# A one-core decoder trunk: squares in x's room, early evictions, finer strand steps, and strand work queued behind the FFN's operations

## The chip, the core and the metric

The kernel runs on one core of one Trainium2 chip. TensorE (PE) multiplies; VectorE (DVE), ScalarE (ACT) and GpSimd (POOL) do the elementwise work; SyncE (SP) and ScalarE issue the DMAs. Each engine runs its own instructions in order and waits on semaphores for the others. The metric is the device time of one execution in microseconds, median of several runs; less is better.

## The reference, cut to what matters

One layer of a hybrid decoder over 2,048 prompt positions and 8 samples, width 1,024, all in float32:

```
h = RMSNorm(x);  z = h @ W_in                 # W_in: 1024 x 2432
A = chunked gMLP(z_u, z_v)     B = S5 state space(z_b)
C = short gated convolution    D = RWKV-7 time mixing (4 heads of 64)
x = x + concat(A, B, C, D) @ W_out
gate, up = split(RMSNorm(x) @ W_gu);  x = x + (silu(gate) * up) @ W_down   # d_ff 2816
y = RMSNorm(x)                                # and the states as outputs
```

## The kernel before

**Pieces.** The positions are cut into four pieces `q` of 512 columns; the samples ride with one of them as 8 further columns. Activations lie transposed, features on partitions. A float32 product is made of three passes: operands are split in a rounded part (`hi`) and a bfloat16 rest (`lo`), and `mmg` (L272) emits hi*hi (L281), then lo*hi and hi*lo (L286). `weights` (L224) loads half a weight tile into a `raw` buffer (three of them), rounds it on ACT (L240), and either makes its rest on DVE (L244, the first time, and stores it) or loads the rest stored before (L242).

**Stages.** For piece 0, `norm0` loads x, scales it into `h` and starts the sum of squares; `m.columns()` (`zrw`) makes the seven z tiles of RWKV, the first four of which wait in PSUM (`mm`, four buffers) for the norm's factor `rs0`, which `zload` multiplies in (L790). `zrest` makes the other ten. Then for q = 1, 2, 3 `norm1(q)` (L403) and `park(h, q, n1)` (L749) compute all z tiles of that piece and store them to HBM (`zdr`), so that later `zload` only loads them. `norm1` loads each x tile into a buffer of the pool `gz` (tag "t", six buffers, shared with z tiles, with the park's `zp` and with the FFN's ft, gp and gr), writes `h` into ring side 1 (`put_gain`, L380), and squares x into a tile of tag "raw" (L415), the weights' own three buffers; `squares` (L302) adds four of these on POOL (L313) and the last three on DVE (L317, L319). `Rms`/`rms` (L327) then make 1/rms: matmuls with ones (L338), a square root on ACT, a reciprocal on DVE, a Newton step (L290) on POOL or DVE, and matmuls that broadcast it (L354).

**Main stream.** For each piece: `outphase` (W_out), `norm2`, `ffn`, and for the first three `final`. In `ffn`, `up(f)` is two weight tiles of matmuls (gate, up), `gated` (L1436) takes them through DVE gp, ACT tanh, POOL gr, DVE ft twice, ACT ah and DVE al (L1445 to L1451), and `down` adds products into x on DVE (L1464).

**Strands.** Work that is not a large matmul is written as generators. `tick` (L127) counts PE work (1 for a matmul of 512 columns); each `Strand` sleeps for as many ticks as it yields and then emits its next step in the middle of the main stream's matmuls. PE's order is this emission order, by hand. The order on DVE, ACT, POOL and the DMA queues is made by a list scheduler: in its own model of time it takes the ready instruction with the highest priority (main stream 8000, RWKV strand `RP` 4000, others `MP` 3500; among equals the earlier emitted). While the FFN of piece q runs, the strands of piece q+1 run: `Mix.rwkv` (two halves of `rw_a` to `rw_d`, with a triangular inverse of 30 dependent steps on POOL, L1256 to L1261) and `Mix.others` (`zrest`, gMLP, S5), which starts in the FFN at `i == 3`. In `zrest` for a parked piece everything up to the first `yield 0` is one step: 15 or 16 loads from `zdr` and their elementwise work. For piece 0, `s5_setup` (L506) makes tables with long chains on POOL (its powers in L651 to L677 use the same scratch `inv_` as the inverse), and eight rounds of PE transposes (L711) that need POOL copies (L699).

## Time and profile before

| | |
|---|---|
| three runs, median | 2643.06 us (2640.42 to 2652.55) |
| the profiled execution | 2647.65 us, its span 2645.9 us |
| TensorE clock granted over it | 0.955 of full |
| busy in the span | PE 92%, DVE 53%, ACT 40%, POOL 30% |

The span is the time between the first and the last instruction of the profile; the execution's own time is 1.75 us longer. PE is busy nearly always, so that what can be saved is its idle time and the stretches in which its clock was granted at half. Stages by the trace: piece 0's columns and the rest of its z tiles to 145 us, the three parks to about 640 us, then four rounds of `outphase` and FFN; strands run beside the first three, to about 2185 us.

### The profile page before, as it was taken

The page shows a single profiled execution, that of the slowest core. Times are in us where ns is not written, and L with a number is a line of the kernel's source. Part 1 is how long each engine was busy: PE and PEld are TensorE (multiplying, and loading weights), DVE is VectorE, ACT ScalarE, POOL GpSimd, SP SyncE. Part 2 cuts the span into 40 slices and gives each one's busy share as a digit, 9 for nine tenths or more (in the row PEclk, how much of TensorE's full clock was granted, in tenths as well). Part 3 has the DMA queues.
Part 4 walks back from the last instruction along what each step waited for, and adds up shares of the span by engine and source line. Part 5 has one row for each costly group of instructions (what it writes and reads, how often), then busy time and mean ns, then how long its engine had stood idle before and what let it go on. Part 6 is the DMA issues. An engine that isn't in the chain of part 4 may idle for free.

```text
span 2645.9 us, 39723 instructions
## 1 busy us (share of the span) xinstructions
PE 2422.5 (92%) x13857; PEld 1622.9 (61%) x14020; DVE 1414.7 (53%) x2790; ACT 1045.6 (40%) x2118; POOL 792.0 (30%) x1267
## 2 busy tenths in 40 slices
PE   7949979799979999999899999997999999999997
PEld 3638846555545556545466565554665558888886
DVE  6943233333788776656755554557555543333334
ACT  4542243433453333345533333544343435322223
POOL 6085116201263262032621711426235113100001
PEclk8978989899989999999999999998999999999999
DMA  5334546555444444464434544634444346444443
GB/s 170 112 115 145 174 133 192 162 155 181 120 126 126 134 138 129 131 185 141 147 120 125 156 128 138 214 110 146 128 135 145 109 141 203 130 134 134 137 138 99
DMA packets 285320, 375.86 MB, mean 142 GB/s; under 512 B 50968, under 2 KB 160576, under 8 KB 285120
## 3 DMA queue, kind: packets, MB, share of 16 engines
q1 hardware_dynamic: 239568, 323.19, 40.4%
q10 hardware_dynamic: 45552, 50.14, 5.4%
q8 instruction: 110, 1.80, 0.3%
q14 instruction: 90, 0.74, 0.1%
HBM read 318.89 MB, written 54.31 MB: 141 GB/s over the span
## 4 chain that ended last, share of the span: by engine, by line
PE 68%; POOL 10%; DVE 10%; issue 4%; DMA 4%; ACT 3%; ACTq 0%; SPq 0%; POOLq 0%; DVEq 0%
PE m L286 38%; PE m L281 21%; POOL BD L1261 3%; POOL inv L1259 3%; DMA z<-zdr 1%; PE x L1229 1%; DVE wl L244 1%; PE x L1305 1%; PE x L1296 1%; PE x L1285 1%; POOL rs L313 1%; POOL s5Q L520 1%; ACT wh L240 1%; DVE U L834 1%; PE ms L717 1%
## 5 line engine op out<-in xcount | busy, mean ns | idle before, releaser
L286 PE MATMUL m<-rl,wh 128*128 128x512 bf16 (+1 forms) x2758 | 847.4, 340 | 13.0 <-DVE rl L384 3.5
L286 PE MATMUL m<-rh,wl 128*128 128x512 bf16 (+1 forms) x2641 | 826.6, 347 | 0.1
L240 ACT CAST wh<-raw 128x512 fp32r<-128x512 f32 x744 | 451.7, 618 | 945.1 <-PE m L286 585.1
L281 PE MATMUL m<-rh,wh 128*128 128x512 f32 (+1 forms) x2760 | 652.5, 377 | 78.7 <-ACT wh L240 63.3
L286 PEld LDWEIGHTS <-wl 128*128 128x128 bf16 x3640 | 353.0, 100 | 350.9 <-issue 106.2
L281 PEld LDWEIGHTS m<-rh,wh 128*128 128x128 f32 x2760 | 455.2, 194 | 177.8 <-ACT wh L240 65.1
L286 PEld LDWEIGHTS <-wh 128*128 128x128 bf16 x3640 | 359.1, 99 | 237.1 <-issue 17.2
L1447 POOL TENSOR_TENSOR gr<-gp,rs 128x512 f32<-128x512 f32 (+1 forms) x110 | 124.9, 1144 | 749.3 <-DVE gp L1445 680.3
L1464 DVE TENSOR_TENSOR xm<-m,xm 128x512 f32<-128x512 f32 (+1 forms) x440 | 246.9, 581 | 128.4 <-PE m L286 119.0
L281 PE MATMUL m<-ah,wh 128*128 128x512 f32 (+1 forms) x880 | 250.8, 401 | 56.7 <-DVE gp L1445 16.0
L286 PE MATMUL m<-al,wh 128*128 128x512 bf16 (+1 forms) x880 | 275.9, 344 | 3.8 <-issue 1.3
L286 PE MATMUL m<-ah,wl 128*128 128x512 bf16 (+1 forms) x838 | 267.5, 351 | 0.7 <-DMA wl<-lod 0.7
L281 PEld LDWEIGHTS m<-ah,wh 128*128 128x128 f32 x880 | 149.2, 193 | 108.0 <-DVE xm L1464 19.1
L1259 POOL TENSOR_TENSOR inv<-BD 32x30 f32<-32x30 f32 (+14 forms) x240 | 132.3, 551 | 197.0 <-DMA BD<-dl 178.8
L244 DVE TENSOR_TENSOR wl<-raw,wh 128x512 bf16<-128x512 f32 x186 | 139.3, 757 | 59.9 <-ACT wh L240 56.4
L1445 DVE TENSOR_TENSOR gp<-m,rs 128x512 f32<-128x512 f32 (+1 forms) x110 | 62.1, 582 | 175.9 <-PE m L286 148.6
L1261 POOL TENSOR_TENSOR BD<-BD,inv 32x30 f32<-32x30 f32 (+14 forms) x240 | 148.4, 618 | 18.2
L1284 POOL TENSOR_SCALAR stl<-st,g 128x64 f32<-128x64 f32 x128 | 68.5, 549 | 276.6 <-DVE st L1299 256.3
L1448 DVE SCALAR_TENSOR_TENSOR ft<-ft,gr 128x512 f32<-128x512 f32 (+1 forms) x110 | 78.7, 730 | 83.6 <-POOL gr L1447 70.6
L1449 DVE SCALAR_TENSOR_TENSOR ft<-ft,m 128x512 f32<-128x512 f32 (+1 forms) x110 | 62.0, 580 | 99.8 <-PE m L286 98.8
L1451 DVE TENSOR_TENSOR al<-ft,ah 128x512 bf16<-128x512 f32 (+1 forms) x88 | 63.2, 718 | 35.9 <-ACT ah L1450 35.3
L757 DVE TENSOR_TENSOR zp<-m,rs 128x260 f32<-128x260 f32 (+1 forms) x68 | 35.8, 554 | 85.3 <-PE m L286 72.7
(378 smaller groups left out, 2677.3 us busy)
## 6 DMA issues: line engine op xcount, KB each, us to landing
raw<-in_wgu SPq DMA_DIRECT2D x352, 256.0 KB, 2.9
wl<-lod SPq DMA_DIRECT2D x558, 128.0 KB, 2.2
raw<-in_wd SPq DMA_DIRECT2D x176, 256.0 KB, 2.9
raw<-in_wz SPq DMA_DIRECT2D x136, 256.0 KB, 2.9
lod<-wl ACTq DMA_DIRECT2D x186, 128.0 KB, 3.2
raw<-in_wo SPq DMA_DIRECT2D x64, 256.0 KB, 3.3
zdr<-zp ACTq DMA_DIRECT2D x40, 256.0 KB, 2.9
z<-zdr SPq DMA_DIRECT2D x40, 256.0 KB, 3.7
```

The costliest lines, as they stand in the source:

```text
L240: S.copy(hi, raw)
L244: V.tensor_tensor(lo, raw, hi.bitcast(F32), op=ALU.subtract)
L281: T.matmul(p_[:, :n], lhsT=wh, rhs=xh[:, c0 : c0 + n], start=i == 0, stop=False)
L286: T.matmul(p_[:, :n], lhsT=a, rhs=b[:, c0 : c0 + n], start=False, stop=e and i == ends[id(ps)])
L1259: G.tensor_tensor(tv, xtv[:, 0:s, s : s + 1].to_broadcast([32, s, r]), xtv[:, s : s + 1, s + 1 :].to_broadcast([32, s, r]), op=ALU.mult)
L1261: G.tensor_tensor(xtv[:, 0:s, s + 1 :], xtv[:, 0:s, s + 1 :], tv, op=ALU.add)
L1284: G.tensor_scalar(stl[:, j], old[:, j], pvw[:, 8 * j + c, 32:33], None, op0=ALU.mult)
L1445: V.tensor_tensor(gp[:, c], pss[0][b][:, :n], rs[:, c], op=ALU.mult)
L1447: G.tensor_tensor(gr[:, c], gp[:, c], rs[:, c], op=ALU.mult)
L1448: V.scalar_tensor_tensor(tv, tv, 1.0, gr[:, c], op0=ALU.add, op1=ALU.mult)
L1451: V.tensor_tensor(al[:, :w], t[:, :w], ah[:, :w].bitcast(F32), op=ALU.subtract)
L1464: V.tensor_tensor(xm[m][:, c0 : c0 + n], p_[:, :n], xm[m][:, c0 : c0 + n], op=ALU.add)
```

## The change

- `Strand.step`: the step's instructions on ACT and DVE are queued behind the main stream's last FFN operation already emitted on that engine (`anchors`): ah on ACT; al, or the last addition of `down`, on DVE. `issue_after` orders the queue of one engine and adds no semaphore.
- `squares` in `norm1` writes the square over x itself, so that "raw" holds weights only; for q = 1 x lies in the two large tiles `big0`, `big1` (which `norm0` used before, and `rw_b` uses after), and `norm1(1)` is emitted right after piece 0's columns instead of after `zrest`.
- The Newton steps of the first norm and of `norm1` go from POOL to DVE.
- In `zrw` for piece 0, the first two z tiles are copied by ACT from PSUM to SBUF before the norm is done, and scaled in place later.
- Steps: `zrest` of a parked piece yields 12 ticks at up to 15 more places; `s5_setup` 28 for 20; `norm2`'s strand waits 48 for 30, `final`'s 100 for 40; `nx.start(36)` for `nx.start(10)`.

```diff
--- before.py
+++ after.py
@@ -93,6 +93,7 @@
     offs = [0]
     strands = []
     now = [0.0]
+    anchors = {}
 
     class hp:
 
@@ -116,7 +117,11 @@
             strands.append(self)
 
         def step(self):
-            with hp(self.prio):
+
+            with ExitStack() as es:
+                es.enter_context(hp(self.prio))
+                for a in anchors.values():
+                    es.enter_context(tc.issue_after(a.ins))
                 d = next(self.gen, None)
             if d is None:
                 self.over = True
@@ -307,8 +312,9 @@
             if k == 0:
                 act(acc[:, :w], xk(k), AF.Square)
                 continue
+            x = xk(k)
             sq = new()
-            act(sq[:, :w], xk(k), AF.Square)
+            act(sq[:, :w], x, AF.Square)
             if not fast or k < 5:
                 G.tensor_tensor(acc[:, :w], acc[:, :w], sq[:, :w], op=ALU.add)
             elif late is None:
@@ -405,23 +411,25 @@
         w = zwidth(q)
         h = ring_tile(1)
 
+        xs = []
+
+        big = [rw.tile([P, 4 * TW], F32, tag=f"big{i}", name=nm("x1")) for i in range(2)] if q == 1 else []
+
         def xk(k):
-            t = zt_("x")
+            t = big[k // 4][:, TW * (k % 4) : TW * (k % 4) + TW] if big else zt_("x")
             nc.sync.dma_start(t[:, :w], I["xq"][q, :, k, :w])
             put_gain(h, k, w, t[:, :w], "n1")
+            xs.append(t)
             return t[:, :w]
 
-        def sq():
-            return wpool.tile([P, TW], F32, tag="raw", bufs=3, name=nm("sq"))
-
-        return h, Rms(squares(xk, w, sq, True), w, prio=MP, wait=64, gap=48)
+        return h, Rms(squares(xk, w, lambda: xs[-1], True), w, V, prio=MP, wait=64, gap=48)
 
     early = [weights([("wz", 0)], (60000, 49999))[0]]
     with hp(20000):
         h, acc0 = norm0()
 
-    first = Rms(acc0, TP, wait=60, prio=18000)
-    rs0 = acc0
+    first = Rms(acc0, TP, V, wait=60, prio=18000)
+    rs0 = acc0[:, :TP]
 
 
     glu = cload("glu", [P, 2, 256])
@@ -703,7 +711,7 @@
                         else:
                             act(cv[ps_, ri, g], bc[ps_, 3, pr], AF.Copy, scale=-1.0)
                             act(fv[ps_, ri, :, g], Ft[ps_, 1, pr], AF.Copy, scale=-1.0)
-                yield 40 if pr == 0 else 20
+                yield 40 if pr == 0 else 28
                 yield from ms_free()
                 pe = mst()
                 pm = pe[:, 256:384]
@@ -782,19 +790,29 @@
     ahead0 = []
 
     def zload(h, m, q, off=0):
-        t = zt_()
         if q in parked:
+            t = zt_()
             nc.sync.dma_start(t[:, off : off + zwidth(q)], zdr[q - 1, m, :, : zwidth(q)])
             return t
-        for p_, (c0, n) in zip(ahead0.pop(0) if ahead0 else ztile(h, m, q), zblocks(q)):
-            V.tensor_tensor(t[:, off + c0 : off + c0 + n], p_[:, :n], rs0[:, c0 : c0 + n], op=ALU.mult)
+        p_ = ahead0.pop(0) if ahead0 else ztile(h, m, q)[0]
+        if m < 2:
+            t, p_ = p_, p_[:, 1:]
+        else:
+            t = zt_()
+        V.tensor_tensor(t[:, off : off + TP], p_[:, :TP], rs0, op=ALU.mult)
         return t
 
     def zrw(h, q):
         w = zwidth(q)
         zs = rw.tile([P, 7, TP], F32, tag="zs", name=nm("zs"))
         if q == 0:
-            ahead0.extend(ztile(h, m, q) for m in range(4))
+
+            for m in range(4):
+                ahead0.append(ztile(h, m, q)[0])
+                if m < 2:
+                    t = zt_()
+                    S.copy(t[:, 1 : TP + 1], ahead0[m])
+                    ahead0[m] = t
             first.done()
 
         for m in range(7):
@@ -829,6 +847,8 @@
             zt = zload(h, 7 + j, q)
             for pr in range(4):
                 src = zt[32 * pr : 32 * pr + 32, :TP].rearrange("p (c s) -> p c s", s=4)
+                if q in parked:
+                    yield 12
                 for s in range(4):
                     e = (S.copy, V.tensor_copy)[s % 2]
                     e(U5[32 * s : 32 * s + 32, 4 * j + pr], src[:, :, s])
@@ -844,6 +864,8 @@
 
         ys = []
         for j in range(2):
+            if q in parked:
+                yield 12
             zx = zload(h, 9 + j, q)
             zz = zload(h, 11 + j, q, 2)
             S.copy(zz[:, 0:2], cc[:, j])
@@ -862,6 +884,8 @@
                                            op0=ALU.mult, op1=ALU.add)
                 nc.scalar.dma_start(O["cvs"][:, j, 0], cbuf[:, j, 1])
                 nc.scalar.dma_start(O["cvs"][:, j, 1], zq)
+            if q in parked:
+                yield 12
             zb = zload(h, 13 + j, q)
             E.tensor_tensor(y[:, :w], y[:, :w], zb[:, :w], op=ALU.mult)
             ys.append(y)
@@ -872,6 +896,8 @@
             wv = [weight("wv", i) for i in range(2)]
         vn = []
         for g, (b0, nb, rows) in enumerate(groups(q)):
+            if q in parked:
+                yield 12
             vt = zt_() if rows == P else vs
             n = 256 * nb
             if q in parked:
@@ -1415,7 +1441,7 @@
             put_gain(h2, k, w, xm[k][:, :w], "n2")
             return xm[k][:, :w]
 
-        return h2, Rms(squares(xk, w, at_, True), w, V, prio=2 * RP, wait=30)
+        return h2, Rms(squares(xk, w, at_, True), w, V, prio=2 * RP, wait=48)
 
     def ffn(h2, scale, xm, q):
         w = width(q)
@@ -1447,8 +1473,8 @@
                     G.tensor_tensor(gr[:, c], gp[:, c], rs[:, c], op=ALU.mult)
                     V.scalar_tensor_tensor(tv, tv, 1.0, gr[:, c], op0=ALU.add, op1=ALU.mult)
                     V.scalar_tensor_tensor(tv, tv, 0.5, pss[1][b][:, :n], op0=ALU.mult, op1=ALU.mult)
-                S.copy(ah[:, :w], t[:, :w])
-                V.tensor_tensor(al[:, :w], t[:, :w], ah[:, :w].bitcast(F32), op=ALU.subtract)
+                anchors["S"] = S.copy(ah[:, :w], t[:, :w])
+                anchors["V"] = V.tensor_tensor(al[:, :w], t[:, :w], ah[:, :w].bitcast(F32), op=ALU.subtract)
             return Split(ah, al, TW)
 
         def down(fs, acts, ws, bl):
@@ -1461,7 +1487,7 @@
                 with hp(EP):
                     for m, (ps, _, _) in zip(range(m0, m0 + g), jobs):
                         for p_, (c0, n) in zip(ps, bl):
-                            V.tensor_tensor(xm[m][:, c0 : c0 + n], p_[:, :n], xm[m][:, c0 : c0 + n], op=ALU.add)
+                            anchors["V"] = V.tensor_tensor(xm[m][:, c0 : c0 + n], p_[:, :n], xm[m][:, c0 : c0 + n], op=ALU.add)
 
         def wdown(fs):
             return weights([("wd", f) for f in fs])
@@ -1508,7 +1534,7 @@
         ts = [gt() for _ in range(KT)]
         for k, t in enumerate(ts):
             act(t[:, :w], xk(k), AF.Copy, scale=col("nf", k))
-        n = Rms(acc, w, prio=2 * RP, wait=40)
+        n = Rms(acc, w, prio=2 * RP, wait=100)
 
         def out():
             yield from wait_for(lambda: n.strand.over)
@@ -1624,13 +1650,15 @@
 
     m = Mix(0, h)
     m.columns()
+    with hp(MP):
+        ahead = norm1(1)
     m.start()
     with hp(MP):
         m.gm2 = m.rest()
         next(m.gm2)
     for q in range(1, npiece):
         with hp(2 * RP):
-            h, n1 = norm1(q)
+            h, n1 = ahead if q == 1 else norm1(q)
         if q == 1:
             m.start_rest(30)
         with hp(2 * RP):
@@ -1640,7 +1668,7 @@
         nx = Mix(q + 1) if q < last else None
         if nx:
             nx.columns()
-            nx.start(10)
+            nx.start(36)
         with hp(2 * RP):
             xm = outphase(m.cct, q)
             h2, scale = norm2(xm, q)
```

## Rows read from the trace of the kernel before

**Rows 1.** The page: the chain that ended last, by engine
```profile
PE 68%; POOL 10%; DVE 10%; issue 4%; DMA 4%; ACT 3%; ACTq 0%; SPq 0%; POOLq 0%; DVEq 0%
```
**Rows 2.** Waits of PE: us in total, times, longest us
```profile
PE m L281 <- ACT wh L240: 70.3, 5, 26.4
PE m L281 <- DVE gp L1445: 16.3, 4, 7.9
PE m L281 <- DVE xm L1464: 15.0, 11, 3.2
PE m L281 <- DVE ft L1449: 10.6, 2, 6.9
PE ms L354 <- POOL rt L296: 9.7, 2, 6.4
PE ms L338 <- DVE rs L319: 8.6, 2, 4.3
...
PE x L1290 <- DVE z L1288: 7.7, 3, 7.1
...
PE ms L338 <- POOL rs L313: 4.2, 2, 3.7
```
**Rows 3.** Timeline of PE: start, us, instruction, [idle before it <- releaser]
```profile
46.24 3.78 PE L281 MATMUL m<-rh,wh 128*128 128x512 f32 x8 [6.75 <-DVE z L790]
...
170.90 0.80 PE L281 MATMUL m<-rh,wh 128*128 128x260 f32 x2 [26.37 <-ACT wh L240]
...
366.49 0.80 PE L281 MATMUL m<-rh,wh 128*128 128x512 f32 x1 [17.95 <-ACT wh L240]
...
518.58 0.79 PE L281 MATMUL m<-rh,wh 128*128 128x512 f32 x1 [19.03 <-ACT wh L240]
```
**Rows 4.** Stretches: us; busy of PE, PEld, DVE, ACT, POOL; granted clock, DMA
```profile
146.80:174.10 27.30, 3.20 (x14) 2.54 (x14) 17.94 (x19) 14.25 (x25) 25.10 (x29) 0.50 0.38 108
187.80:201.40 13.60, 8.58 (x37) 7.45 (x38) 1.53 (x4) 0.75 (x2) 12.36 (x34) 0.50 0.28 89
...
747.60:757.80 10.20, 5.85 (x14) 2.99 (x15) 8.54 (x13) 1.85 (x3) 9.30 (x12) 0.50 0.29 78
...
1307.40:1327.80 20.40, 10.04 (x21) 3.83 (x23) 20.30 (x35) 7.52 (x15) 12.41 (x20) 0.58 0.54 165
...
1816.00:1836.40 20.40, 9.75 (x22) 4.14 (x22) 20.19 (x37) 9.77 (x18) 12.72 (x27) 0.50 0.50 135
```
**Rows 5.** Timeline at the start of park(2), all engines
```profile
361.13 0.71 ACT L188 ACTIVATE rh<-x,c_pv 128x512 fp32r<-128x512 f32 x1
...
363.27 8.32 SPq L237 DMA_DIRECT2D raw<-in_wz  x8
...
375.00 2.21 PE L281 MATMUL m<-rh,wh 128*128 128x512 f32 x8
...
380.40 2.22 PE L281 MATMUL m<-rh,wh 128*128 128x512 f32 x8
```
**Rows 6.** Timeline of POOL: the inverse's first step, then the last of the S5 powers
```profile
134.76 0.23 POOL L1259 TENSOR_TENSOR inv<-BD 32x30 f32<-32x30 f32 x1 [53.51 <-DMA BD<-dl]
...
237.47 0.40 POOL L517 TENSOR_SCALAR inv<-inv 128x256 f32<-128x256 f32 x1
```
**Rows 7.** The transposes of the S5 setup: count, ns min/median/max, first and last start
```profile
L711 PE MATMUL ms<-c_ident,s5R x16: 270/271/273, 237.6 to 307.8; 128*128 128x128 f32 x16
```
**Rows 8.** Stretches of 50 us, columns as in the other stretches
```profile
50.00:100.00 50.00, 49.48 (x219) 27.03 (x222) 47.88 (x114) 28.76 (x68) 3.64 (x10) 0.99 0.36 109
```
**Rows 9.** The page's costliest groups: al, the last operation of a gated tile
```profile
L1451 DVE TENSOR_TENSOR al<-ft,ah 128x512 bf16<-128x512 f32 (+1 forms) x88 | 63.2, 718 | 35.9 <-ACT ah L1450 35.3
```
**Rows 10.** Groups of instructions by line: ACT's table loads
```profile
L188 ACT ACT_TABLE_LOAD x37 | 47.5, 1283 | 19.8 <-DMA z<-zdr 7.7 <-DVE wl L244 3.7 <-DVE z L790 3.1
```
**Rows 11.** Timeline of PE: the last norm, whose Newton step is on DVE
```profile
2632.86 0.80 PE L354 MATMUL m<-c_ident,rt 128*128 128x128 f32 x6 [2.25 <-DVE rt L296]
```
**Rows 12.** The page's DMA issues: KB each, median us from issue to landing
```profile
z<-zdr SPq DMA_DIRECT2D x40, 256.0 KB, 3.7
```

## The prediction

> **What bounds the kernel now.** I read the chain that ended last first: two thirds of it is PE, and the rest is shared by POOL, DVE, DMA and ACT [rows 1]. The reader is to see that PE sets the end and is not always fed. Then the list of PE's waits, which says by whom [rows 2]: weight casts on ACT (70.3 us in only five waits), then DVE operations of the FFN (gp, xm, ft: 41.9 us together), then pieces of the norms. The timeline shows where the five lie: 26.37 us before park(1) restarts, 17.95 and 19.03 us at the starts of park(2) and park(3) [rows 3]. Last come the stretches in which the clock was granted at about half, 1.2 of 2.4 GHz [rows 4]: each follows such an idle time, and half of PE's busy time in it is lost beside the idle time itself.
>
> The cast that ends the long waits is not slow; its load is late. At park(2) the eight raw loads are issued from 363.27 on, only after the norm's squares have left the raw buffers, while the last scaling of x on ACT already ran at 361.13 [rows 5]. So squares and weights compete for the same three buffers.
>
> **The change, part by part.** The sum is made against the profiled execution's 2647.65 us.
>
> *Start (A).* The first two PSUM tiles are emptied by ACT before the norm ends, so the fifth z tile need not wait for the scaling on DVE: 6.75 us of idle [rows 3]. The two added copies run on ACT while PE works on the next tile; without that cover they would cost their own time, about that of al [rows 9]. The Newton step leaves POOL: of 9.7 us in two waits [rows 2], 6.4 belong to q = 1 (below) and 3.3 to this norm; on DVE such a wait is 2.25 [rows 11], 1 saved. A = 8.
>
> *Park(1) (B).* `norm1(1)` moves ahead of `zrest`, with its eight loads on SP, its scalings and squares on ACT, four additions on POOL, and on DVE eight rests, three additions and the Newton step. At park(1) `h` and the factor are then ready and no square holds a raw buffer: 26.37 us [rows 3] and the 6.4 us go, and with them half of 3.20 + 8.58 us at half clock [rows 4], 5.9: 38.7 us in all. What is late next is POOL. Its inverse starts at 134.76 and the S5 powers, which need the same scratch, end at 237.47 + 0.4 [rows 6], 103.1 us later. PE's first setup transposes stand at 237.6 and the eighth at 307.8 [rows 7], 10.0 us apart, so the third round, whose POOL copies are queued behind the powers, stands at about 257.7. Moved up by 38.7 and back by the 2 x 8 added ticks (a 24-tick weight tile took 380.40 - 375.00 = 5.40 us [rows 5], 0.225 a tick: 3.6) it would come at 222.6, 15 us before POOL is done. The squares that leave POOL shorten its chain by a few us. So B lies between 24 and 38.7, and lower if DVE holds the inverse up; I take 26, since POOL's chain is the nearer row.
>
> *Park(2) and park(3) (C).* The weights can now be loaded ahead, so PE starts with the first scaled x instead of after the last and is paced by ACT: the last scaling at 361.13 + 0.71, its rest on DVE, then the last products, say 365. The first tile ended at 375.00 before [rows 5]: 10 us. Park(3) has the same wait within 1.1 us [rows 3], so C = 20; 14 if x's own buffers, now held until POOL has added, delay the last loads, 28 if PE is held up less than ACT's pace says.
>
> *Bursts in three FFNs (D).* `zrest` of a parked piece comes as one step; it lands on `rw_elem`, and in that stretch DVE is busy 20.30 of 20.40 and 20.19 of 20.40 us [rows 4]. Fourteen or fifteen yields of 12 ticks spread it over some 170 ticks, 38 us. On offer are the waits for gp, xm, ft and z, 49.6 us [rows 2], and at the reduced clock 5.85 x 0.50 + 10.04 x 0.42 + 9.75 x 0.50 = 12 us [rows 4]. I take three quarters of gp and z (18), nothing of xm and ft, since a strand's step that is emitted before those operations is not held behind them, and half of the clock (6): D = 24, between 5 and 61.
>
> *Norms in the main stream (E, F).* `norm2`'s matmul waits 4.3 us twice for the last additions [rows 2]; 18 more ticks are 4 us. That saves 8.6. In the last piece, however, the factor is asked for after 48.75 ticks, so both its steps then fall together and PE waits as in the last norm, 2.25 [rows 11]. E = 6. `final`'s 60 ticks cover its 4.2 us [rows 2]: F = 4. They also put off the next RWKV strand by 60 x 0.225 = 13 us, hidden as long as the strand ends before the FFN does.
>
> *Prices.* The anchors (G): a strand operation emitted just after a gated tile now waits for its ft, ah and al, some 2 us (three operations like the 0.72 us of al [rows 9]), while PE asks for RWKV's result 10 ticks (2.2 us) later. Of the 3 x 16 x 3 such waits about one in eight falls there (2 us of the 72 ticks, 16 us, between gated tiles), 18 of 144, each costing PE between nothing and 2 us: 0 to 36, and possibly a gain. I take 4, near the low end, as the gap covers the wait. Earlier `norm1(1)` (H): DVE is busy 47.88 of 50 us between 50 and 100 [rows 8], where some of its dozen operations of about 0.72 us [rows 9] land, 0 to 9; 3 taken, as most find room before 50.
>
> *Table loads (I).* A load of ACT's function table took 1.283 us, 37 times on one line [rows 10]. In `zrest` the gelu and the square root of each group now stand apart, with the FFN's tanh between: some four more loads per piece, twelve in all, 15 us of an engine that is 40% busy: 0 to 15, 3 taken. The Trainium skill (ScalarE: Activation LUTs, What ACT_TABLE_LOAD costs) puts a drain beside the load, 2.66 us for a switch, and so speaks against finer steps; by it the twelve would be 32 us and the term, by the same share, an estimated 6. The load itself agrees with the row; the drain is not a row here.
>
> Sum: 8 + 26 + 20 + 24 + 6 + 4 - 4 - 3 - 3 = 78. 2647.65 - 78 = 2569.7. The profiled execution stands 4.6 us above the median of the runs, so the forecast is **2565 us**.
>
> **Rivals.**
> *POOL takes over (R1).* B and D fall to what POOL's chains allow. For: POOL is a tenth of the chain already [rows 1], and its inverse does not get shorter. Against: in the FFNs the inverse has hundreds of ticks of room. B at 12 and D at 5 take 33 from the sum: 2598.
> *The yields do nothing for PE (R2).* The scheduler places by its own clock, so the spread strand may stand before gp and xm as before, and the anchors bind nothing that stood in front. For: the xm waits come in ones all over the S5 steps (11 of them [rows 2]). Then D and its prices G and I are gone: 78 - 24 + 7 = 61 saved, 2582.
> *Slower: buffers of `gz` (R3).* Finer steps hold two conv results and the gMLP tiles of six buffers across yields, while each gated tile needs three; a gated tile then waits for a strand's tile, which waits for its load and its anchored operation. The price is at most a load's 3.7 us [rows 12] at each of 3 x 14 steps: 155 us against the other parts' 54 (without D), 101 us slower at worst; at half of it, 78, the loss is 24 and the time 2667. It decides from 54 / 42 = 1.3 us a step on. Against: only some of the steps meet a gated tile, and PE has 5.4 us of the next weight tile to work on.
>
> **How the numbers follow.** Forecast 0.50, R1 0.18, R2 0.14, gains beyond the forecast (D near its upper bound) 0.06, R3 0.06, and 0.06 for R3's mechanism at about 1.3 us a step, which gives no change. About 0.5% of the time, 13 us, is what a measurement of this kernel can tell from no change; R1 and R2 both lie beyond it, on the fast side: faster 0.88, same 0.06, slower 0.06. The range takes the upper bounds of B and C and half of D's way to its own (13 + 8 + 18 more: 2526, and a little below), and reaches past R1 with G at 18 and H and I at their upper ends (14 + 6 + 12 more: 2630, and a little inside). So 2520 to 2626.
>
> **What would show it.** In the changed profile the three casts before the parks should be gone from PE's waits, park(1) starting at once and park(2), park(3) within 5 us; the clock whole between 147 and 174; the DVE stretches of the bursts well under 90% busy; L338 no longer waiting on DVE in `norm2`; a new wait of PE on the POOL copies in the S5 setup of up to 15 us. The forecast is wrong if PE waits in the FFNs for ft, gp or z have grown, if SP's raw loads there stand behind loads of z, or if a park still waits for its weights.

## The result, and the profile after

The changed kernel took 2567.98 us (median of 4 runs, 2564.37 to 2575.41) beside 2642.25 us (2640.42 to 2652.55) of the kernel before on the same chip: a ratio of 0.9715, 95% interval 0.9682 to 0.9748. The forecast was 2565 us, and faster. The sum was right within 6 us of 78; most of its terms were not, and the misses went in both directions.

The page of the changed kernel, whose span is 2573.6 us (2645.9 before): the engines' busy time, and the chain that ended last, which here follows only the last part of the span and is not used further.

```profile
PE 2410.5 (94%) x13856; PEld 1617.8 (63%) x14020; DVE 1419.6 (55%) x2810; ACT 1052.8 (41%) x2125; POOL 794.8 (31%) x1247
...
PE 22%; DVE 1%; ACT 1%; issue 0%; POOL 0%; POOLq 0%; DVEq 0%; ACTq 0%
```

PE idles 163 us of the span. Its waits (us in total, times, longest), which answer to [rows 2]:

```profile
PE m L286 <- ACT rh L193: 19.8, 10, 5.2
PE m L286 <- DVE xm L1490: 15.0, 11, 2.8
PE ms L360 <- issue: 9.8, 1, 9.8
...
PE ms L725 <- ACT s5es L721: 7.0, 8, 3.3
...
PE x L1316 <- DVE z L1314: 6.4, 6, 1.6
PE m L286 <- DVE ft L1475: 6.4, 2, 4.3
PE ms L938 <- DVE z L950: 5.9, 1, 5.9
...
PE m L360 <- DVE rt L301: 4.5, 2, 2.3
PE m L286 <- DVE gp L1471: 4.4, 3, 1.6
```

The 70.3 us behind weight casts have gone down to 1.3 us in one wait. gp has fallen from 16.3 to 4.4 and ft from 10.6 to 6.4, xm not at all. New are 9.8 us in front of L360, the broadcast of the first norm, and 5.9 us in front of L938, a product of the gMLP in FFN 0. The wait for ACT's scalings of x (rh) has grown from 5.5 to 19.8 us. The timeline of PE says where these lie (start, us, instruction, idle before it); it answers to [rows 3].

```profile
45.88 2.05 PE L360 MATMUL ms<-c_ident,rt 128*128 128x128 f32 x8 [9.80 <-issue]
...
149.21 0.58 PE L286 MATMUL m<-rh,wh 128*128 128x260 f32 x2
...
317.38 0.80 PE L286 MATMUL m<-rh,wh 128*128 128x512 f32 x1 [4.93 <-ACT rh L193]
...
458.75 0.80 PE L286 MATMUL m<-rh,wh 128*128 128x512 f32 x1 [5.18 <-ACT rh L193]
...
2176.97 1.13 PE L360 MATMUL ms<-c_ident,rt 128*128 128x128 f32 x8 [1.48 <-DVE rt L301]
...
2181.02 3.62 PE L286 MATMUL m<-rh,wh 128*128 128x260 f32 x15 [1.20 <-DVE gp L1471]
```

park(1) starts at 149.21 with no wait before it (26.37 us before), park(2) and park(3) after 4.93 and 5.18 us (17.95 and 19.03 before). So the three long gaps fell about as forecast.

To see where the 72.3 us between the two spans come from, I cut both executions at the first product of each stage, which is the same instruction in both, and read each stretch. A gap just ahead of a stage counts in the stage before it; the last stage ends with PE's last instruction, 7 us before the end of the span in both.

| stage | before, us (PE busy) | after, us (PE busy) | gain, us |
|---|---|---|---|
| norm and z tiles of piece 0 | 170.9 (122.95) | 149.2 (124.84) | 21.7 |
| park(1) | 195.6 (162.33) | 168.2 (152.34) | 27.4 |
| park(2) | 152.1 (130.48) | 141.4 (130.80) | 10.7 |
| park(3) | 119.4 (117.04) | 125.2 (120.47) | -5.8 |
| output phase 0 | 53.4 (48.64) | 52.6 (47.10) | 0.8 |
| FFN 0 | 473.9 (437.89) | 478.0 (440.39) | -4.1 |
| output phase 1 | 54.3 (50.12) | 46.3 (46.08) | 8.0 |
| FFN 1 | 458.5 (431.17) | 451.8 (428.23) | 6.7 |
| output phase 2 | 48.2 (47.20) | 46.3 (46.03) | 1.9 |
| FFN 2 | 467.7 (437.45) | 457.7 (433.73) | 10.0 |
| output phase 3 | 46.3 (46.30) | 46.3 (46.30) | 0.0 |
| FFN 3 and the end | 398.3 (390.91) | 403.4 (394.21) | -5.1 |

The rows behind it are stretches like these (us; busy of PE, PEld, DVE, ACT, POOL with instructions; granted clock, DMA). They are park(1), FFN 1, FFN 3, then the stretch that answers to the first of [rows 4], and the fullest 20.40 us of DVE in FFN 1 and in FFN 2.

```profile
149.20:317.40 168.20, 152.34 (x1247) 134.64 (x1245) 62.66 (x148) 52.42 (x139) 87.89 (x203) 0.94 0.53 164
...
1160.90:1612.70 451.80, 428.23 (x2107) 257.42 (x2145) 267.89 (x494) 194.85 (x386) 150.55 (x228) 0.98 0.46 139
...
2163.00:2566.40 403.40, 394.21 (x3215) 342.89 (x3213) 154.70 (x365) 120.05 (x231) 40.23 (x55) 0.98 0.42 129
...
146.80:174.10 27.30, 27.30 (x221) 22.51 (x220) 19.66 (x29) 14.45 (x25) 24.55 (x36) 1.00 0.50 156
...
1250.40:1270.80 20.40, 15.28 (x59) 7.29 (x59) 20.18 (x28) 4.70 (x10) 15.72 (x28) 0.92 0.47 148
1748.20:1768.60 20.40, 14.03 (x53) 7.53 (x53) 20.16 (x28) 4.72 (x10) 15.72 (x28) 0.92 0.44 139
```

The stretch from 146.8 is now full on PE at the whole clock (3.20 of 27.30 us at half before). The last two rows are worth a second look: DVE is busy 20.18 and 20.16 of 20.40 us, as in the bursts of [rows 4], yet PE works 15.28 and 14.03 us instead of 10.04 and 9.75, at a granted clock of 0.92 for 0.58 and 0.50. At its fullest DVE is as full as before; the order of its work has changed. DVE's timeline in FFN 2, between 1743 and 1754, shows it: the additions to xm, for which PE waits, stand between the strand's copies.

```profile
1743.83 1.34 DVE L854 COPY U<-z 32x128 f32<-32x128 f32 x2
1745.20 1.29 DVE L1490 TENSOR_TENSOR xm<-m,xm 128x512 f32<-128x512 f32 x2
...
1747.08 0.92 DVE L854 COPY U<-z 32x128 f32<-32x128 f32 x2
...
1749.62 0.66 DVE L1490 TENSOR_TENSOR xm<-m,xm 128x512 f32<-128x512 f32 x1
```

In the kernel before, DVE's timeline of the same burst has no operation of the main stream between these two, 13 us apart, only operations of `zrest` and of the RWKV strand:

```profile
1813.27 0.68 DVE L1451 TENSOR_TENSOR al<-ft,ah 128x512 bf16<-128x512 f32 x1
...
1826.83 0.67 DVE L1445 TENSOR_TENSOR gp<-m,rs 128x512 f32<-128x512 f32 x1
```

**The new wait in the first norm.** All engines of the changed kernel between 39.8 and 46 us, shortened to the chain that ends in it:

```profile
39.82 1.28 POOL L319 TENSOR_TENSOR rs<-rs,x 128x520 f32<-128x520 f32 x1
...
42.56 0.26 POOL L525 TENSOR_SCALAR t<-t 128x8 f32<-128x8 f32 x1
...
42.85 0.21 ACT L193 ACTIVATE t<-t 128x8 f32<-128x8 f32 x1 [6.41 <-POOL t L525]
42.96 0.60 ACT L245 CAST wh<-raw 128x512 fp32r<-128x512 f32 x1
...
43.60 0.69 DVE L249 TENSOR_TENSOR wl<-raw,wh 128x512 bf16<-128x512 f32 x1 [7.77 <-ACT wh L245]
...
45.62 0.16 DVE L301 TENSOR_TENSOR rt<-rt,s 128x4 f32<-128x4 f32 x1
```

Read it upwards. PE waits for the Newton step's last operation (45.62). DVE reaches that late because a weight's rest (43.60) stands ahead of it on its queue and waited 7.77 us for the cast on ACT (42.96). The cast stands behind a sine of the S5 setup (42.85), which waited 6.41 us for POOL. And POOL was late because four additions of `norm1(1)` of some 1.28 us, now emitted early, came between the setup's small operations. No engine is short of time here: POOL's 1.28 us pass through the queues of ACT and DVE to PE. The last link is a matter of the order on DVE. In e1 below, whose start has the same program but another order by the scheduler, the additions stand at the same place and a sine waits even longer for POOL, but the Newton step stands ahead of the held-up rest, and PE waits 1.20 us:

```profile
39.90 1.30 POOL L317 TENSOR_TENSOR rs<-rs,x 128x520 f32<-128x520 f32 x1
...
43.44 0.21 ACT L191 ACTIVATE t<-t 128x8 f32<-128x8 f32 x1 [7.35 <-POOL t L523]
...
37.55 1.13 PE L358 MATMUL ms<-c_ident,rt 128*128 128x128 f32 x8 [1.20 <-issue]
```

**POOL in park(1).** The chain of [rows 6] and the transposes of [rows 7], first the timeline of POOL, then the line of the transposes.

```profile
144.74 0.23 POOL L1285 TENSOR_TENSOR inv<-BD 32x30 f32<-32x30 f32 x1 [54.11 <-DMA BD<-dl]
...
210.83 1.09 POOL L707 COPY s5R<-s5G 64x64 f32<-64x64 f32 x4
...
225.51 1.09 POOL L707 COPY s5R<-s5G 64x64 f32<-64x64 f32 x4
...
239.44 0.41 POOL L525 TENSOR_SCALAR inv<-inv 128x256 f32<-128x256 f32 x1
```

```profile
L719 PE MATMUL ms<-c_ident,s5R x16: 270/271/284, 207.2 to 289.8; 128*128 128x128 f32 x16
```

PE's setup moved up by 30.4 us (237.6 to 207.2) while the powers ended 2 us later than before (239.44 against 237.47). Yet nothing waits: the POOL copies that the transposes need stand among the powers, at 210.83 and 225.51, not behind them.

### The profile page after: what moved, and what is told of

It reads as the page before. It is cut to its first block, busy times and chain, and to the rows that moved or that the text cites. A ratio compares the mean times of both kernels' runs of the same rounds, so it can differ in the third digit from the quotient of the medians.

```text
span 2573.6 us, 39717 instructions
## 1 busy us (share of the span) xinstructions
PE 2410.5 (94%) x13856; PEld 1617.8 (63%) x14020; DVE 1419.6 (55%) x2810; ACT 1052.8 (41%) x2125; POOL 794.8 (31%) x1247
## 5 line engine op out<-in xcount | busy, mean ns | idle before, releaser
L286 PE MATMUL m<-rh,wh 128*128 128x512 f32 (+1 forms) x2760 | 647.2, 375 | 33.2 <-ACT rh L193 19.8
L286 PE MATMUL m<-ah,wh 128*128 128x512 f32 (+1 forms) x880 | 245.4, 396 | 25.2 <-DVE xm L1490 10.1
L1285 POOL TENSOR_TENSOR inv<-BD 32x30 f32<-32x30 f32 (+14 forms) x240 | 140.7, 586 | 233.8 <-DMA BD<-dl 215.6
L1287 POOL TENSOR_TENSOR BD<-BD,inv 32x30 f32<-32x30 f32 (+14 forms) x240 | 140.1, 584 | 18.2
L319 POOL TENSOR_TENSOR rs<-rs,at 128x512 f32<-128x512 f32 (+1 forms) x41 | 56.0, 1366 | 76.9 <-ACT at L193 74.9
```

The source lines that it names most:

```text
L286: T.matmul(p_[:, :n], lhsT=wh, rhs=xh[:, c0 : c0 + n], start=i == 0, stop=False)
L1285: G.tensor_tensor(tv, xtv[:, 0:s, s : s + 1].to_broadcast([32, s, r]), xtv[:, s : s + 1, s + 1 :].to_broadcast([32, s, r]), op=ALU.mult)
L1287: G.tensor_tensor(xtv[:, 0:s, s + 1 :], xtv[:, 0:s, s + 1 :], tv, op=ALU.add)
```

## The experiments

How far a single stage can be trusted: the kernel e4 below has the same order of instructions on PE, DVE and ACT as the changed one up to the last FFN, and its stages up to there differ by up to 3.3 us in length. A difference below that in a single long stage shows nothing by itself (output phases 1 and 2 repeat better: 46.3 us in all kernels with the new ticks); the ratios, each to runs of the kernel before on the same chip, decide.

### The FFNs: anchors and yields

**e1**, the changed kernel without the anchors.

```
-                for a in anchors.values():
-                    es.enter_context(tc.issue_after(a.ins))
```

> The changed kernel without the anchors: a strand's step is emitted as before the change, all else as changed. The changed kernel took 2568 us. Theory 1: in the FFNs the anchors take as much as they give. They keep gp and ft from waiting (PE's waits for these two fell from 26.9 to 10.8 us), but PE now waits for strand operations that are queued behind al: 5.9 us for the gMLP of the samples and some 12 us more for RWKV's uv, z and st. Then this run lies within 6 us of the changed kernel, with those waits gone and those for gp and ft back. Theory 2: the anchors are what holds the gain in FFN 1 and FFN 2, and without them the run is 10 to 20 us slower. Theory 3: they only cost; 10 us or more faster.

**e2**, without the yields in `zrest` (each of the five places as this one).

```
-                if q in parked:
-                    yield 12
                 for s in range(4):
...
```

> The changed kernel with zrest of a parked piece as one step again (the yields of 12 ticks left out), anchors kept. Theory 1 (the forecast's term D): the burst fills DVE, and spreading it is what shortens FFN 1 and FFN 2; the run is 10 to 20 us slower than the changed kernel's 2568, with PE waiting for gp and xm in the stretch after i == 3 of each FFN. Theory 2: with the anchors the burst can no longer stand in front of a gated tile, so the spread matters little: within 5 us.

**e5**, without both.

> The changed kernel without the anchors and with zrest as one step: the FFNs' strands as before the change but for their starting ticks. Leaving out the yields alone cost some 18 us, the anchors alone some 6. Theory 1: the two parts add, and this run is 20 to 28 us slower than the changed kernel. Theory 2: the two need each other (anchored bursts stand together behind one operation and then hold up the next additions into x: PE's wait for xm grew from 15.0 to 32.5 us in the run with one step), so that without both the loss is smaller than with the anchors alone: 5 to 15 us.

| kernel | ratio to before (95%) | median, us | FFN 0, 1, 2, us |
|---|---|---|---|
| changed | 0.9715 (0.9682 to 0.9748) | 2567.98 | 478.0, 451.8, 457.7 |
| e1, no anchors | 0.9738 (0.9717 to 0.9758) | 2578.31 | 473.1, 454.6, 461.2 |
| e2, no yields | 0.9784 (0.9765 to 0.9803) | 2589.81 | 479.0, 457.9, 465.4 |
| e5, neither | 0.9822 (0.9808 to 0.9837) | 2598.05 | 472.5, 461.3, 472.2 |

PE's waits in e1, e2 and e5, the rows that moved:

```profile
PE m L284 <- DVE ft L1473: 23.9, 4, 7.7
...
PE x L1314 <- DVE z L1312: 11.9, 7, 3.7
```

```profile
PE m L286 <- DVE xm L1482: 32.5, 15, 8.4
```

```profile
PE m L284 <- DVE xm L1480: 21.4, 14, 5.2
...
PE m L284 <- DVE gp L1461: 16.7, 5, 6.3
```

The yields are worth 0.0069 of the time, 18 us (e2 against the changed kernel, intervals apart); the profiled spans differ by 13.1 us, nearly all in FFNs 1 and 2 (6.1 and 7.7 us). Without them PE waits for xm twice as long, 32.5 us, though DVE is no fuller: its fullest 20.40 us in FFN 1 of e2 are

```profile
1232.90:1253.30 20.40, 11.90 (x50) 6.35 (x48) 19.68 (x33) 12.50 (x29) 14.20 (x20) 0.89 0.52 154
```

The anchors are worth 0.0038, 10 us, where there are no yields (e5 against e2, intervals apart). Beside the yields they bring 0.0023, 6 us, which the intervals do not settle; the wait for ft is 6.4 us with them and 23.9 without. Both left out cost 28 us, a little more than the 24 of each left out alone. In no pair do the anchors cost anything over the whole. In FFN 0 alone both kernels without them are about 5 us shorter, and the list of PE's waits shows a price there: the 5.9 us in front of L938 at 818.15. An operation of 0.28 us on DVE (L950, part of the samples' gMLP) comes at 817.82, behind `al` (814.61) and four operations of the RWKV strand. The wait is gone in e1 and e5; it is gone in e2 too, whose FFN 0 is no shorter, so it is not the whole of that price.

### The start: the early norm1

**e3**, the changed kernel with the first norm's Newton step back on POOL.

```
-    first = Rms(acc0, TP, V, wait=60, prio=18000)
+    first = Rms(acc0, TP, wait=60, prio=18000)
```

> The changed kernel with the first norm's Newton step back on POOL. In the changed kernel PE waits 9.8 us for this norm, because the five small operations on DVE stand behind a weight's rest that waits for a cast on ACT, and that stands behind a sine that waits for POOL's setup chain, into which the early squares' additions were put. Theory 1: the Newton step on DVE is what is held up; on POOL, at a high priority, it is done within the 3.3 us of before: 5 to 7 us faster than 2568. Theory 2: the crowd on POOL and ACT is what holds it up, and on POOL it waits as long: within 2 us.

0.9726 (0.9702 to 0.9751), 2575.31 us: no difference from the changed kernel. The broadcast waits 11.06 us, now for POOL. Where the Newton step stands does not matter while the queues ahead of it are held up.

**e6**, `norm1(1)` held behind the last shift of piece 0's columns (on DVE) and its last copy (on ACT).

```
-    with hp(MP):
+    with hp(MP), tc.issue_after(ends['V'].ins), tc.issue_after(ends['S'].ins):
         ahead = norm1(1)
```

> The changed kernel with norm1(1) queued on ACT and DVE behind the last operation of piece 0's columns, so that its squares can't run among the first norm. In the changed kernel PE waits 9.8 us before the first norm's broadcast, and at the 136th hi*hi matmul it is 4.9 us behind the kernel before. Theory 1: the early norm1(1) is what crowds the first norm; with it behind, the wait is 3 us or less, PE is some 8 us earlier at the 68th matmul, and of this 3 to 8 us are left at the end. Theory 2: the delay comes from elsewhere, and the wait stays near 10 us. If theory 1 holds but the work now collides with piece 0's columns on a full DVE, the gain at the 68th matmul is gone by the 168th.

0.9753 (0.9738 to 0.9769), 2580.72 us. The timeline of PE, at the first norm and at the sums of `norm1(1)`:

```profile
36.17 1.13 PE L360 MATMUL ms<-c_ident,rt 128*128 128x128 f32 x8 [1.01 <-issue]
...
91.34 2.26 PE L344 MATMUL ms<-c_ones,rs 128*128 128x1 f32 x10 [17.68 <-DVE rs L325]
```

The wait of 9.80 us is gone, 1.01 left, and PE is 10 us ahead of the changed kernel: so without the early additions nothing holds up the first norm (with them, e1 shows, it still depends on DVE's order). But now `norm1(1)` comes late for its own sums, which PE asks for after 64 ticks, and 17.68 us are lost there.

**e10** is e6 with these sums asked for later.

```
-        return h, Rms(squares(xk, w, lambda: xs[-1], True), w, V, prio=MP, wait=64, gap=48)
+        return h, Rms(squares(xk, w, lambda: xs[-1], True), w, V, prio=MP, wait=210 if q == 1 else 64, gap=48)
```

> As the run with norm1(1) queued behind the columns, and in addition its matmuls with ones 210 ticks later instead of 64, so that PE does not wait 17.7 us for the sum of squares as it did there. Theory 1: that wait was the only price of the later place; PE keeps the some 10 us gained at the 68th hi*hi matmul in good part, and the run is 3 to 8 us faster than the changed kernel. Theory 2: DVE is full between 50 and 145 us, and the gain is paid back there as in the run with the start alone (10 us gained, 2 left): within 2 us of the changed kernel.

0.9731 (0.9707 to 0.9754), 2573.66 us: no gain over the changed kernel. The wait of 17.68 us is gone, but at the 136th product PE is 8.5 us behind the changed kernel, of which it makes up half in park(1). PE's timeline has two other waits instead, for a weight's rest on DVE and for an activation on ACT:

```profile
81.24 0.61 PE L291 MATMUL m<-rh,wl 128*128 128x512 bf16 x1 [7.64 <-DVE wl L249]
...
98.92 2.07 PE L1134 MATMUL x<-g,c_blk 128*128 128x512 f32 x2 [9.22 <-ACT g L193]
```

**e7**, the kernel before with only the start's two edits: the early copies of two z tiles, and the first Newton step on DVE.

```
-    first = Rms(acc0, TP, wait=60, prio=18000)
+    first = Rms(acc0, TP, V, wait=60, prio=18000)
...
+                if m < 2:
+                    t = zt_()
+                    S.copy(t[:, 1 : TP + 1], ahead0[m])
+                    ahead0[m] = t
```

> The kernel before the change with the start's part alone: the two early copies from PSUM and the first norm's Newton step on DVE. Theory 1 (term A of the forecast): without the early norm1(1) this saves some 8 us at the 68th hi*hi matmul, and the wait of 6.75 us on the scaling is gone. Theory 2: the copies or the Newton step cost as much by themselves, 0 to 2 us. What is left of it at the end can be less, since the park waits for POOL and its loads anyway.

0.9994 (0.9982 to 1.0005), 2643.59 us: nothing. The early copies do what they should: at the 34th product PE is 10.0 us ahead of the kernel before, and the wait for z is 2.38 us instead of 6.75. By the 136th 2.8 us are left and 2.0 at the end of park(1), at whose start PE still waits 26.50 us for the first weight. DVE is busy 49.43 of 50 us between 50 and 100 (47.88 before [rows 8]), and time won ahead of that stretch comes back in it or just behind it, in waits such as 3.39 us for ACT and 2.86 for DVE:

```profile
50.00:100.00 50.00, 46.52 (x201) 25.73 (x202) 49.43 (x110) 28.93 (x63) 4.08 (x10) 0.97 0.42 126
```

**e8**, the changed kernel with `norm1(1)` at its old place (the x tiles in the ring of z tiles; the squares still in x's own room).

```
-    with hp(MP):
-        ahead = norm1(1)
...
-            h, n1 = ahead if q == 1 else norm1(q)
+            h, n1 = norm1(q)
```

> The changed kernel with norm1(1) where it was before the change, after zrest, its x in the z tiles' pool; the square still takes x's room. This parts term B: what the early norm1(1) brings and what the freed raw buffers bring. Theory 1: as in the other parks the freed buffers alone end the wait for the cast, and PE is paced by ACT's scalings, so that of the 26.4 us before park(1) some 6 stay, and the norm's 6.4 us stay too in part: 8 to 15 us slower than the changed kernel. Theory 2: POOL, busy with the inverse, holds the squares and with them x's buffers, so that the loads of x are late as before: 20 us or more slower. Theory 3: the early place brings nothing at all, since it is paid back at the start: within 4 us.

0.9802 (0.9786 to 0.9818), 2592.27 us: 23 us slower than the changed kernel. park(1) now waits several times for the scaled x, and ACT's scalings for the loads of x, as theory 2 had it (what held up the loads was not looked at):

```profile
148.54 0.80 PE L286 MATMUL m<-rh,wh 128*128 128x260 f32 x2 [7.43 <-ACT rh L193]
...
159.53 0.73 ACT L193 ACTIVATE rh<-x,c_pv 128x520 fp32r<-128x520 f32 x1 [4.03 <-DMA x<-in_xq]
...
160.31 0.80 PE L286 MATMUL m<-rh,wh 128*128 128x260 f32 x2 [4.52 <-ACT rh L193]
```

At the 136th product PE is 8.5 us ahead of the changed kernel here, 2.5 of them because the products of `norm1(1)` itself come later; at the 204th it is 31.7 us behind, by the end of park(1) 19.2. So of what park(1) won, about 19 to 25 us come from the early `norm1(1)`, and the rest, which remains here, from the other edits, among them the squares that no longer hold raw buffers.

### The other ticks, and the last norm

**e9**, the old ticks for the next RWKV strand (10) and for `final` (40).

```
-        n = Rms(acc, w, prio=2 * RP, wait=100)
+        n = Rms(acc, w, prio=2 * RP, wait=40)
...
-            nx.start(36)
+            nx.start(10)
```

> The changed kernel with the strands' old starting ticks: nx.start(10) and 40 ticks for final's norm. Without anchors and yields FFN 1 and FFN 2 of the changed kernel took 461.3 and 472.2 us, longer than the 458.5 and 467.7 of the kernel before, though norm2's later matmul should have saved 4.3 us in each. Theory 1: the later ticks move the RWKV strand onto zrest and are what cost these 7 to 9 us per FFN, so with the old ticks FFN 1 and FFN 2 are 5 to 9 us shorter each, outphase 1 is some 8 us longer (final's wait for POOL is back), and the run is 2 to 10 us faster. Theory 2: the later ticks are needed beside the anchors (RWKV's first step then is emitted behind the first gated tiles), and the run is 5 us or more slower. Theory 3: they do no more than remove final's wait: 5 to 10 us slower, all of it in the outphases.

0.9719 (0.9693 to 0.9745), 2572.25 us: no difference. Output phases 1 and 2 are 4.0 and 1.2 us longer than in the changed kernel, and FFN 2 7.4 shorter; FFN 0 (3.1 longer) and FFN 1 (1.9 shorter) lie within what executions differ by. What the later strand saves in the output phases comes back later in the FFNs.

**e4**, the changed kernel with `norm2`'s old wait in the last piece.

```
-        return h2, Rms(squares(xk, w, at_, True), w, V, prio=2 * RP, wait=48)
+        return h2, Rms(squares(xk, w, at_, True), w, V, prio=2 * RP, wait=30 if q == last else 48)
```

> The changed kernel with 30 ticks instead of 48 for norm2 of the last piece alone. In the changed kernel the last FFN is 5.0 us longer than before; PE waits 1.5 and 1.2 us there and its clock is at half for 6.8 us. Theory: both steps of the norm fall together at 48.75 ticks and that is the whole of it: this run is 4 to 5 us faster than 2568. Rival: something else in that FFN is longer, and the run is the same.

0.9696 (0.9675 to 0.9718), 2566.29 us. The last FFN is 398.4 us long (403.3 in the changed kernel, 398.3 before). In the changed kernel the first of the two waits shown above, 1.48 us, is followed by a stretch at half clock, in which the second, 1.20 us, lies; its row:

```profile
2177.90:2184.90 7.00, 5.12 (x23) 4.40 (x23) 3.18 (x7) 3.39 (x6) 1.60 (x2) 0.52 0.00 0
```

In e4 the only waits there are 0.68 and 0.25 us and the granted clock stays 1.00 from 2172 to 2182.7. The medians' difference is inside the intervals; the stage's is 4.9 us and was seen in all three kernels that have the old wait.

**e11** is e10 and e4 together, with the anchors emptied in FFN 0 behind every gated tile and every down product. **e12** is the changed kernel with only these last two.

```
+                if q == 0:
+                    anchors.clear()
```

> The run before it, with two more edits: norm2's wait of the last piece at 30 ticks (alone 5 us in the last FFN), and no anchors in FFN 0 (there the run without anchors was 4.9 us shorter). If the three are independent, 10 to 17 us faster than the changed kernel; 5 to 10 if the start's gain is paid back by a full DVE. Rival: without anchors in FFN 0 the strand's steps only move, and the gain there is within 2 us.

> The changed kernel with two of its parts taken back where the earlier runs showed a loss: norm2's wait is 30 ticks again in the last piece (48 in the others), and the anchors are emptied behind every gated tile and every down product of the first FFN, so that they act in FFNs 1 and 2 alone. Theory 1 (the losses are local and add): the last FFN is 403.3 - 4.9 = about 398.4 us long, FFN 0 about 473 (478.0 in the changed kernel), all else stays, and the whole is some 10 us shorter than the changed kernel, about 2558 us, ratio 0.968. Theory 2 (the order of the strand's steps in FFN 0 decides what falls into outphase 1 and the FFNs behind it, so what FFN 0 gains comes back later): FFN 0 is shorter, but outphase 1 and FFN 1 are together longer by about as much, and only the 5 us of the last FFN stay: about 2563, ratio 0.970.

e11: 0.9712 (0.9685 to 0.9739), 2571.53 us. e12: 0.9688 (0.9672 to 0.9705), 2565.6 us. Their last FFNs are 398.4 and 398.9 us long, and FFN 0 is 4.0 and 3.5 us shorter than in the changed kernel, without the 5.9 us in front of L938. In e12, FFN 1 is 3.3 longer and park(2) 4.4, and its span is 2569.0, 4.6 us shorter than the changed kernel's: what theory 2 said in size, though the time comes back in other stages than it named. Fewer anchors also change DVE's order from the start of the kernel on, so FFN 0's gain is not a local one. The ratios of e4 and e12 are the lowest of all kernels here, but their intervals overlap with the changed kernel's, so that either beats it by 5 us is likely and not shown.

## Why the prediction was right

The parts as the stages show them, in the order of the sum: at the 136th product PE is 5.0 us behind, by the end of park(1) 36.1 ahead, after park(3) 54.0. Of the 5.0 us, 2.5 are work that has moved: the 20 products of `norm1(1)`'s norm (1.17 + 1.05 + 0.28 us), which PE did in park(1) before and now does ahead of that product. They belong to neither term, so they are taken out of both.

| part | forecast, us | measured, us | from |
|---|---|---|---|
| A, H start, with the early norm1 | 8 - 3 | -2.5 | -5.0 + 2.5 at the 136th product |
| B park(1) | 26 | 38.6 | 36.1 + 2.5 |
| C park(2), park(3) | 20 | 17.9 | 54.0 - 36.1 |
| D, G, I strands in the FFNs | 24 - 4 - 3 | 4.0 | -4.1 + 6.7 + 10.0 - 8.6 of norm2 |
| E norm2 | 6 | 3.5 | 8.6 - 5.1 |
| F output phases | 4 | 10.7 | 0.8 + 8.0 + 1.9 |
| sum | 78 | 72.2 | |

**A and H failed, and in sign.** The early copies do shorten the wait for z (6.75 to 2.38 us; e7 is 10.0 us ahead), but e7 also shows that of the 8 us only 2.8 are left at the 136th product, behind a DVE that is full until 100: the step that failed is "6.75 us of idle" counted as won, although the row for DVE stood in the prediction [rows 8]. H was sized by DVE's operations alone, at 3. e7 and the changed kernel lie 7.8 us apart at that product; less the 2.5 of moved work, 5.3 us are the price of the early `norm1(1)`, inside its range of 0 to 9. The prediction listed POOL's four additions and put them to no cost; in the changed kernel they hold up PE by 9.80 us in front of the broadcast. e3 excludes the Newton step as the cause, and in e6 the wait is gone with the early place. But that wait is not where the price is paid: e1 and e12 have 1.20 and 2.06 us there, are 8 us ahead of the kernel before at the 34th product, and at the 136th as far behind as the changed kernel (5.2 and 5.4 us). Which queue takes the 5.3 us was not followed. Nor is the wait a lever: without it (e1, e6, e10, e12) the time is the same or longer.

**B was too small**: 38.6 is its upper bound of 38.7, the sum of the waits and the half clock without a price for POOL. The step that failed is R1's premise, on which 26 was chosen: "the third round, whose POOL copies are queued behind the powers". The scheduler, which orders POOL's work anew, put the copies between the powers, so POOL's chain set no limit, though it ended where it did before.

**C was right**, and its mechanism with it: the starts of park(2) and park(3) wait for a scaling on ACT, 4.93 and 5.18 us, no longer for a weight cast; park(2) was said to begin with the first scaled x. These two waits alone shrank by 13.0 and 13.9 us, nearer to the upper 28; 9.0 us of that come back inside the two parks, behind their starts: further short waits for scalings, and a granted clock of 0.78 over the first 21.3 us of park(3).

**D was the wrong size, for a reason that the sum lacked.** Yields are worth 18 us (e2), close to the 17 of D with its prices, and anchors are a gain, 10 us without yields, where G was a price of 4. But the price that G named exists as well: the 5.9 us in front of L938 in FFN 0, and with it the wait for z, which was to be a sign against the forecast, has grown in the FFNs from 7.7 to 12.3 us (6.4 + 5.9). The gain of the yields agrees with the mechanism, and excludes R2: PE's wait for xm is 32.5 us without yields and 15.0 with them. But the sum took xm and ft as untouched and gp as the gain, and took for granted that without D the FFNs would stay as they were. They do not: with neither (e5), FFNs 1 and 2 are 2.8 and 4.5 us longer than before in spite of the 8.6 us that norm2 no longer waits, some 16 us worse. Another part of the change costs that; e9 points to the strand that starts 26 ticks later, since FFNs 1 and 2 are together 9.3 us shorter with the old ticks, but FFN 0 is 3.1 longer there and the whole the same. That it is the ticks and nothing else was not tried in e5's setting and stays open. That DVE would be "well under 90% busy" was also wrong: at its fullest it is 20.18 of 20.40 us with the yields and 19.68 without, so what the yields changed is the order of its work and not how full it is.

**I** was put at twelve added loads of ACT's tables; the groups by line of the changed kernel have 41 for the 37 of [rows 10], at the same 1283 ns:

```profile
L193 ACT ACT_TABLE_LOAD x41 | 52.6, 1283 | 20.7 <-DMA z<-zdr 6.8 <-DVE wl L249 5.7 <-DVE g L1203 4.2
```

With one more on the other line of loads, 22 for 21, that is five, 6.4 us of an engine that is busy 41% of the span. The row shows the load's own time; a drain beside it, as the Trainium skill has it (ScalarE: Activation LUTs, What ACT_TABLE_LOAD costs), is no row of this profile either.

**E** had the right gain in FFNs 1 and 2: the two waits for `norm2`'s additions are gone. In the last piece the prediction gave 2.25 us for both steps falling together; it was 5.1. The waits are 1.48 and 1.20 us, together near that, and half of PE's 5.12 us of work at the lower clock comes on top (2.68 + 2.56 = 5.2, less the 0.25 that e4 waits too): the idle time was priced, the clock with it was not, though [rows 4] showed that pair. **F** was too small: output phases 1 and 2 lost 9.9 us, where `final`'s wait of 4.2 alone was counted. With the old ticks (e9) 4.7 of the 9.9 stay, so 5.2 belong to the ticks; e9 shows that these are no net gain. What made the rest stays open.

**The rivals.** R1 did not happen (no wait on POOL in the S5 setup; PE waits 7.0 us for ACT's s5es, 8.2 before). R2 is excluded by e2. R3's waits of a gated tile for a strand's tile are not in PE's list: what PE waits for in the FFNs, ft, gp and xm, has shrunk or stayed, and what z waits for in the one wait that is new is `al` and the RWKV strand on DVE's queue, not a buffer. The total came out close because B and F were 19 us too low and A, C, D and E 25 us too high. That is luck in the sum, and a range that was wide enough for it.

## What to carry to other kernels

Price an early step on every queue that it enters, in order, and follow what each queued instruction releases: here four additions on an engine that is a third busy reached TensorE through the queues of two others, in one order of the scheduler and not in another. Where a scheduler places the work, the order in the trace of before is no bound for the order after, in either direction; put the likelier value between the bounds and not at the pessimistic one. When strands compete with the main stream on a full engine, look not at its busy share but at which instruction stands in front of the one that TensorE waits for: finer steps, with the engine as full as before, moved 18 us here.

## What the runs showed of the hardware

Short waits can cost about as much in clock as in themselves: waits of PE of 1.48, 0.68 and 1.20 us stand close together in the last FFN, PE ran at 1.2 GHz for 6.8 us from 2178.1 on, behind the first of them, and the last FFN was 4.9 us longer than in e4, which has 0.68 and 0.25 us there and an unbroken clock of 2.4 GHz. And two executions with the same order of instructions differ by up to 3.3 us in a single stage of some 450 us while their spans up to the last FFN differ by 2.2 us (2163.0 and 2160.8), so one profile of each kernel is not enough to judge a part that is worth less.
